# Turning the feed-forward activations on VectorE instead of TensorE, in a two-layer hybrid decoder trunk

## The chip, the cores and the metric

The kernel runs on one core of one Trainium2 chip. The metric is the device time of one execution in microseconds (us). TensorE (PE) multiplies matrices, VectorE (DVE) and ScalarE (ACT) work element by element, GpSimd (POOL) does small jobs and issues some DMAs, and SyncE (SP) issues the loads of the weights. Every engine has its own instruction queue and works through it in order.

## The reference

256 tokens of width 2048 pass through two layers, each a token mixer (gated DeltaNet in layer 0, HGRN2 in layer 1) followed by a SwiGLU feed-forward layer with 5632 inner columns. All arrays are float32. What matters here is the feed-forward layer:

```python
def swiglu(h, w_gate, w_up, w_down):
    return (jax.nn.silu(h @ w_gate) * (h @ w_up)) @ w_down
...
for layer in range(DEPTH):
    ...
    h = h + swiglu(rmsnorm(h, ffn_norm[layer]), ffn_w_gate[layer], ffn_w_up[layer], ffn_w_down[layer])
return rmsnorm(h, final_norm)
```

## The kernel before, in words

**Products of split numbers.** Every float32 operand x is kept as two rounded numbers of the type fp32r, a high part h (x rounded) and a low part l (x - h, rounded), and a product is made of three matmuls: high by high, high by low, low by high. For activations these are the tiles `xt_h`/`xt_l` (input of a layer's first products) and `hth`/`htl` (input of the down projection; the profile's names for `ht` and `lt` in the code). For weights they are `wh`/`wl`.

**The stream of weights.** `stream` walks through all weights in halves of 128x1024 elements (512 KB). SyncE loads a half into one of four `raw` buffers, ScalarE rounds it into `wh`, VectorE subtracts to give `wl` (four split buffers, `SPLIT_BUFS`), and TensorE uses it. In the feed-forward layers each half is used by 12 matmuls with 512 columns (`mm_rows`: two slices of the contraction, two halves of the tokens, three products).

**The feed-forward layer** (`ffn`). There are 22 groups of 256 inner columns, done in two parts of 12 and 10 groups (`FF_PARTS`). A group of gate and up is eight weight halves and fills a PSUM tile `main` (one of two) with tokens on the partitions. When it is complete, `end` runs for both token halves: ScalarE takes the Silu of the gate half into `sg`, and VectorE multiplies the up half by the token's scale and `sg` into `h1` (`h` in the profile). The down projection needs these activations with the inner columns on the partitions. So after every second group, eight 128x128 blocks are transposed on TensorE against the identity (`head` in the profile) into two PSUM banks (`aux`, four in all), and from there split: ScalarE rounds them into `ht`, VectorE subtracts into `lt`. Eleven such pairs make a layer, 22 the kernel. After each part come four groups of the down projection, one for each 512 output columns; each runs over all pairs of that part in order.

**The order of the work.** The program records every operation first (class `Recorder`; this is why nearly every row of the profile has the line L490, the one place that issues them). `plan` then computes an order for each engine: an operation has a price (`COST`; for a VectorE transpose of n elements per partition 0.18 + 0.001 n us, times 1.02), a due time counted back from the main matmuls that need it, and an engine takes the ready operation with the earliest due time. Main matmuls keep their order. The buffers of a tile are taken in that simulated time too. On the chip each engine then follows this fixed order and waits on semaphores.

## Time and profile before

| | |
|---|---|
| median of 3 runs | 2809.66 us (2809.59 to 2812.17) |
| profiled execution, its own time | 2811.11 us |
| span of its instructions | 2809.4 us |
| mean granted TensorE clock | 0.997 |

The profile has one row for each group of equal instructions: line, engine, operation, the names of output and inputs, shapes, count, then busy time in us and the mean of one in ns, and the idle time of that engine before them with the instruction whose end ended it. The chain of work that ended last is followed back from the last instruction, so that a piece of it is time which something would have to replace or remove to change the end. In timeline rows the first number is the start and the second the length, both in us.

### The profile page before, as it was taken

What the parts mean: (1) busy time and instruction counts of PE and PEld (TensorE: products, weight loads), DVE (VectorE), ACT (ScalarE), POOL (GpSimd) and SP (SyncE); (2) the same over time, 40 slices, a digit from 0 to 9 for tenths busy, and PEclk for the clock granted to TensorE, in tenths of its full rate; (3) what the DMA queues carried; (4) which work ended last, traced back from release to release, by engine and by line L of the source; (5) the groups of instructions that cost most, each with busy time, mean ns of one, the idle gap of its engine ahead of it and who ended that gap; (6) DMA issues with size and microseconds to landing.
All of it is one profiled execution on the core that took longest, in us unless ns stands there. A gap on an engine that the chain in (4) does not pass through costs nothing.

```text
span 2809.4 us, 41241 instructions
## 1 busy us (share of the span) xinstructions
PE 2788.2 (99%) x15902; PEld 2376.0 (85%) x15902; DVE 1752.2 (62%) x2543; ACT 1422.0 (51%) x1984; POOL 255.1 (9%) x370
## 2 busy tenths in 40 slices
PE   9999999999999999999999999999999999999998
PEld 9988888888888888888888989988888888888887
DVE  6777888877765545444555687678655454454554
ACT  6646666564554444334444556556454444344443
POOL 1212222223110000000000100000110000000000
PEclk9999999999999999999999999999999999999999
DMA  7686678678776556666556655545775656766564
GB/s 255 198 274 201 197 229 255 209 224 254 230 248 206 192 187 189 224 224 191 190 189 218 214 164 168 170 157 168 235 266 189 192 189 204 224 206 191 189 200 159
DMA packets 162677, 580.54 MB, mean 207 GB/s; under 512 B 20138, under 2 KB 21306, under 8 KB 162352
## 3 DMA queue, kind: packets, MB, share of 16 engines
q1 hardware_dynamic: 138912, 503.15, 55.8%
q0 software_dynamic: 23280, 73.91, 8.4%
q8 instruction: 124, 2.03, 0.3%
q10 hardware_dynamic: 288, 0.85, 0.1%
q14 instruction: 73, 0.60, 0.1%
HBM read 550.52 MB, written 27.31 MB: 206 GB/s over the span
## 4 chain that ended last, share of the span: by engine, by line
PE 98%; issue 0%; ACT 0%; DVE 0%; POOLq 0%; POOL 0%; ACTq 0%
PE main L490 91%; PE aux L490 7%; ACT dec L490 0%; DVE wl L490 0%; ACT wh L490 0%; DVE u L490 0%; ACT xt_h L490 0%; DVE utmp L490 0%; DVE pre L490 0%; ACT y L490 0%; POOLq L1748 0%; ACT junk L490 0%; DVE xl L490 0%; POOL coll L490 0%; DVE xt_l L490 0%
## 5 line engine op out<-in xcount | busy, mean ns | idle before, releaser
L490 DVE TENSOR_TENSOR wl<-raw,wh 128x1024 fp32r<-128x1024 f32 x945 | 1161.4, 1230 | 958.9 <-ACT wh L490 955.9
L490 ACT ACTIVATE wh<-raw 128x1024 fp32r<-128x1024 f32 x945 | 1000.5, 1060 | 1280.2 <-PE main L490 1229.3
L490 PE MATMUL main<-wh,xt_h 128*128 128x512 f32 x2176 | 852.0, 392 | 0.6 <-ACT wh L490 0.6
L490 PE MATMUL main<-wl,xt_h 128*128 128x512 f32 x2176 | 850.4, 391 | 0.9 <-DVE wl L490 0.9
L490 PE MATMUL main<-wh,xt_l 128*128 128x512 f32 x2176 | 850.5, 391 | 0.0
L490 PEld LDWEIGHTS main<-wl,xt_h 128*128 128x128 f32 x2176 | 409.6, 188 | 84.7 <-DVE wl L490 1.3
L490 PEld LDWEIGHTS main<-wh,xt_h 128*128 128x128 f32 x2176 | 409.5, 188 | 84.7 <-ACT wh L490 1.0
L490 PEld LDWEIGHTS main<-wh,xt_l 128*128 128x128 f32 x2176 | 409.5, 188 | 84.5
L490 PE MATMUL main<-xt_h,wl 128*128 128x256 f32 (+1 forms) x1040 | 292.2, 281 | 1.6 <-DVE wl L490 1.6
L490 PE MATMUL main<-xt_l,wh 128*128 128x256 f32 (+1 forms) x1040 | 291.8, 281 | 0.3 <-DVE xt_l L490 0.3
L490 PE MATMUL main<-xt_h,wh 128*128 128x256 f32 (+1 forms) x1040 | 290.3, 279 | 0.0
L490 PE MATMUL main<-wh,hth 128*128 128x512 f32 x664 | 258.7, 390 | 0.0
L490 PE MATMUL main<-wh,htl 128*128 128x512 f32 x664 | 258.6, 389 | 0.0
L490 PE MATMUL main<-wl,hth 128*128 128x512 f32 x664 | 258.3, 389 | 0.0
L490 PEld LDWEIGHTS main<-xt_h,wh 128*128 128x128 f32 (+1 forms) x1040 | 195.6, 188 | 0.3
L490 PEld LDWEIGHTS main<-xt_h,wl 128*128 128x128 f32 (+1 forms) x1040 | 193.8, 186 | 2.2 <-DVE wl L490 2.0
L490 PEld LDWEIGHTS main<-xt_l,wh 128*128 128x128 f32 (+1 forms) x1040 | 193.8, 186 | 0.9 <-DVE xt_l L490 0.5
L490 PE MATMUL main<-wl,ot_h 128*128 128x512 f32 x384 | 150.8, 393 | 0.0
L490 PE MATMUL main<-wh,ot_l 128*128 128x512 f32 x384 | 150.6, 392 | 0.0
L490 PE MATMUL main<-wh,ot_h 128*128 128x512 f32 x384 | 150.5, 392 | 0.0
L490 PEld LDWEIGHTS main<-wh,htl 128*128 128x128 f32 x664 | 124.7, 188 | 25.9
L490 PEld LDWEIGHTS main<-wh,hth 128*128 128x128 f32 x664 | 124.7, 188 | 25.8
(207 smaller groups left out, 2203.0 us busy)
## 6 DMA issues: line engine op xcount, KB each, us to landing
raw<-in_ffn_gu SPq DMA_DIRECT2D x352, 512.0 KB, 4.6
raw<-in_ffn_d SPq DMA_DIRECT2D x176, 512.0 KB, 4.6
raw<-in_hgrn_in SPq DMA_DIRECT2D x128, 512.0 KB, 3.9
raw<-in_gdn_kq SPq DMA_DIRECT2D x64, 512.0 KB, 5.0
raw<-in_gdn_v SPq DMA_DIRECT2D x64, 512.0 KB, 4.6
raw<-in_gdn_z SPq DMA_DIRECT2D x64, 512.0 KB, 5.0
raw<-in_gdn_out SPq DMA_DIRECT2D x64, 512.0 KB, 4.6
x_home<-x POOLq DMA_DIRECT2D x36, 512.0 KB, 5.7
```

The lines of the kernel that those rows point to most:

```text
L490: getattr(getattr(tc.nc, op.eng), op.method)(*args, **kw)
```

## The change

The activations of two groups now share one `h1` tile of 128x2x512 (two buffers instead of four of half the size). VectorE turns it: a transpose instruction of VectorE turns each 32x32 block of its operand, and one instruction takes the blocks from one quarter of the partitions (32 of 128) to another, eight blocks at a time (128x2x512 has 16 combinations of a source quarter and a target quarter, so there are 16 instructions for a pair). The result lies in a new SBUF tile, `turned`. The rounding on ScalarE and the subtraction on VectorE then read `turned`, with one instruction each for the whole pair instead of two. The transposes on TensorE for these tiles and the use of two `aux` banks for them are gone.

```diff
+    def turn(self, out, x):
+
+        out = out.rearrange("p n (t a s) -> p t n a s", t=2, s=32)
+        x = x.rearrange("p t (n b s) -> p t n b s", n=4, s=32)
+        for a in range(4):
+            for b in range(4):
+                self.nc.vector.transpose(
+                    out[32 * b : 32 * b + 32, :, :, a, :], x[32 * a : 32 * a + 32, :, :, b, :]
+                )
...
             def end(ps):
-                h1 = self.tile(self.pool, [P, 2, T], "h1", bufs=4)
+                if gi % 2 == 0:
+                    h1s[gi // 2] = self.tile(self.pool, [P, 2, 512], "h1", bufs=2)
+                h1 = h1s[gi // 2]
                 for tt in range(2):
...
                     nc.vector.scalar_tensor_tensor(
-                        out=h1[:, tt, :], in0=ps[:, tt, T:512], scalar=col, in1=sg,
-                        op0=ALU.mult, op1=ALU.mult,
+                        out=h1[:, tt, gi % 2 * T : (gi % 2 + 1) * T], in0=ps[:, tt, T:512], scalar=col,
+                        in1=sg, op0=ALU.mult, op1=ALU.mult,
                     )
-                h1s[gi] = h1
                 if gi % 2 == 0:
                     return
-                pair = hts[gi // 2] = tuple(
+                turned = self.tile(self.pool, [P, 4, T], "turned", bufs=2)
+                self.turn(turned, h1)
+                hts[gi // 2] = ht, lt = tuple(
                     self.tile(self.pool, [P, 4, T], f"ht{x}", F32R, bufs=max(FF_PARTS) // 2) for x in "hl"
                 )
-                two = self.aux(), self.aux()
-                nc.together(*two)
-                for of, tr in enumerate(two):
-                    for k in range(2):
-                        for tt in range(2):
-                            nc.tensor.transpose(
-                                tr[:, k * T + tt * P : k * T + (tt + 1) * P],
-                                h1s[gi - 1 + of][:, tt, k * P : (k + 1) * P], self.ident,
-                            )
-                for of, tr in enumerate(two):
-                    ht, lt = (t[:, 2 * of : 2 * of + 2, :].rearrange("p a t -> p (a t)") for t in pair)
-                    nc.scalar.activation(ht, tr, AF.Copy)
-                    nc.vector.tensor_tensor(out=lt, in0=tr, in1=ht.bitcast(F32), op=ALU.subtract)
+                nc.scalar.activation(ht, turned, AF.Copy)
+                nc.vector.tensor_tensor(out=lt, in0=turned, in1=ht.bitcast(F32), op=ALU.subtract)
```

## The prediction

> **What bounds the kernel now.** I read the engines' busy times first, then the chain that ended last, then the groups with shapes kept apart, then the timeline of single pairs, and last the waits of the DMA queue.

> ```profile
> span 2809.4 us, 41241 instructions
> PE 2788.2 (99%) x15902; PEld 2376.0 (85%) x15902; DVE 1752.2 (62%) x2543; ACT 1422.0 (51%) x1984; POOL 255.1 (9%) x370
> ...
> PE 98%; issue 0%; ACT 0%; DVE 0%; POOLq 0%; POOL 0%; ACTq 0%
> ```

> TensorE is the bound nearly everywhere: it is busy for 99% of the span and is 98% of the chain that sets the end. VectorE idles 38% of the time. So the question of this change is what TensorE time leaves the chain, and whether VectorE, loaded with the work instead, ever makes TensorE wait. The two feed-forward layers in the chain, in order of time (start, length, work; the eleven pieces of the first layer's pairs run from the first row to the tenth, and the last row is the last pair of the second layer):

> ```profile
> 891.58 0.87 PE aux L490 x8
> 892.45 43.54 PE main L490 x192
> 935.99 0.87 PE aux L490 x8
> 936.86 43.54 PE main L490 x192
> 980.40 0.88 PE aux L490 x8
> 981.28 43.54 PE main L490 x192
> 1024.82 0.87 PE aux L490 x8
> ...
> 1466.27 0.88 PE aux L490 x8
> ...
> 2695.15 0.87 PE aux L490 x8
> ```

> The reader is to see a metronome. Two groups of gate and up are 192 matmuls in 43.54 us, 0.2268 us each; then eight transposes take 0.87 us; and nothing lies between. The period of a pair is 44.41 us (935.99 less 891.58). One weight half is 12 matmuls, 2.72 us.

> ```profile
> L490 DVE TENSOR_TENSOR wl<-raw,wh 128x1024 fp32r<-128x1024 f32 x945 | 1161.4, 1230 | 958.9 <-ACT wh L490 955.9
> L490 ACT ACTIVATE wh<-raw 128x1024 fp32r<-128x1024 f32 x945 | 1000.5, 1060 | 1280.2 <-PE main L490 1229.3 <-issue 11.3 <-PE aux L490 8.3
> ...
> L490 DVE TENSOR_TENSOR htl<-aux,hth 128x512 fp32r<-128x512 f32 x44 | 28.2, 682 | 0.0
> ...
> L490 ACT ACTIVATE hth<-aux 128x512 fp32r<-128x512 f32 x44 | 23.5, 587 | 0.0
> ...
> L490 PE MATMUL aux<-head,h 128*128 128x128 f32 x176 | 22.8, 272 | 0.0
> ...
> L490 DVE STREAM_TRANSPOSE inv<-u 32x256 f32<-32x256 f32 x32 | 13.8, 432 | 1.8 <-DMA u<-u_dram 0.6 <-ACT u L490 0.4
> ```

> The columns are the count, the busy time, the mean of one in ns, and the idle time before them. wh and wl are the rounded weight half and its remainder, made on ScalarE and VectorE for every half of the stream: 1.06 and 1.23 us. The 176 transposes are the 22 pairs by eight. The DeltaNet layer already has VectorE transposes of the size that the change adds, 32x256 in f32.

> **The change, step by step.** (1) *Removed from TensorE*: 22 batches of eight transposes. Each batch takes 0.87 us of the chain, with the switch into it and out of it, since the main matmuls on both sides are complete (192 in 43.54 us, with the first slow matmul after a switch inside). 22 x 0.87 = 19.1 us, or 19.2 us with the two or three that show 0.88. All of it lies on the path, because TensorE waits for nothing there. The row of the group offers two other sums: 22.8 us busy (1.04 a batch, which overlaps the neighbouring matmuls), and 176 x 272 ns = 47.9 us (durations of instructions that overlap in the pipeline). I take the chain's number, which is a distance between neighbours.

> [...]

> (2) *Added to VectorE*: 16 transposes of 32x256 per pair, 352 in all. The nearest rows are three in a row in the DeltaNet layer:

> ```profile
> 196.86 1.36 DVE L490 STREAM_TRANSPOSE inv<-u 32x256 f32<-32x256 f32 x3
> 198.25 0.19 DVE L490 TENSOR_TENSOR u<-u,utmp 128x29 f32<-128x29 f32 x1
> ```

> That is 0.453 us each, start to start. So a pair costs 16 x 0.453 = 7.25 us. The new ones have one more level of stride on each side; the trace has no such instruction. From below I bound one by 0.19 us (the small sum above), from above by 1.23 us (the wl row, a VectorE instruction of four times as many elements on each partition). I take 0.453, the row of the same operation, size and type.

> (3) *Changed on VectorE and ScalarE*: two subtractions of 128x512 (2 x 682 ns) become one of 128x1024 from SBUF (1.23 us like wl), and two rounding copies of 128x512 (2 x 587 ns) become one of 128x1024 (1.06 us like wh): 0.1 us less per pair on each engine. VectorE's busy time rises by 22 x (16 x 0.432 + 1.23 - 1.36) = 149 us, to some 1901 us; a pair's window holds

> ```profile
> 891.58:935.99 44.41, 44.41 (x202) 36.86 (x201) 22.39 (x22) 19.41 (x22) 0.00 (x0) 1.00 0.60 191
> ```

> 22.39 us of VectorE in 44.41 now, and 22.4 + 7.25 - 0.1 = 29.5 in 43.54 after, 68%. ScalarE stays at 19.3. The granted clock here is 1.00 and has nothing to give.

> (4) *What covers the added 7.25 us.* VectorE runs in order, and behind the turns stand the wl subtractions that TensorE needs. The steady state:

> ```profile
> 1478.08 1.06 ACT L490 ACTIVATE wh<-raw 128x1024 fp32r<-128x1024 f32 x1 [1.66 <-PE main L490]
> 1480.80 1.06 ACT L490 ACTIVATE wh<-raw 128x1024 fp32r<-128x1024 f32 x1 [1.66 <-PE main L490]
> ...
> 1476.45 1.23 DVE L490 TENSOR_TENSOR wl<-raw,wh 128x1024 fp32r<-128x1024 f32 x1 [1.49 <-ACT wh L490]
> 1479.17 1.23 DVE L490 TENSOR_TENSOR wl<-raw,wh 128x1024 fp32r<-128x1024 f32 x1 [1.49 <-ACT wh L490]
> ```

> wh starts when TensorE has left a split buffer, wl ends 2.32 us later (1478.08 to 1480.40), and with four buffers (SPLIT_BUFS) that half is wanted three halves after the release, 8.2 us: wl may be 5.8 us late before TensorE notices. VectorE idles 1.49 us in each half before wl; three turns (1.36 us) fit into it without moving wl, so the 16 need some six halves of the 16 that a pair has. If one starts just as wl becomes ready, wl is 0.45 us late. A late wl also returns its raw buffer late:

> ```profile
> raw<-in_ffn_gu SPq DMA_DIRECT2D x352, 512.0 KB, 4.6
> SPq L490 <- DVE wl L490: 1908.9, 772, 12.8
> ```

> SP waits on wl for its next load, which lands 4.6 us later (1485.0 for the wl above) and is wanted four halves after its predecessor's wh (1488.96): 3.9 us to spare. Both covers hold if wl slips by 0.5 us. If they were gone, each microsecond of lateness beyond 5.8 would be one on the chain, per pair.

> (5) *Added wait*: the ScalarE copy of a pair waits for all 16 turns, and wh stands behind it in ScalarE's queue; the subtraction then waits for the copy, with wl behind. Priced alike: a copy put too early would delay wh out of the same 5.8 us. The order (plan) ranks work by due time, and the turned pair is due only in the down projection.

> (6) *Where the due time is near*: the last pair of the second part of each layer. Its down group starts while the pair is still being made:

> ```profile
> 1460.66 0.39 PE L490 MATMUL main<-wh,hth 128*128 128x512 f32 x1
> ...
> 1463.10 0.87 DVE L490 SCALAR_TENSOR_TENSOR h<-main,rstd,sg 128x256 f32<-128x256 f32 x2
> 1464.67 1.23 DVE L490 TENSOR_TENSOR wl<-raw,wh 128x1024 fp32r<-128x1024 f32 x1 [0.71 <-ACT wh L490]
> ```

> The last pair is used from the ninth half on, 1460.66 + 8 x 2.72 = 1482.4. From 1463.97, one turn fits before the wl of 1464.67 and three after each wl: the last ends near 1478.3, the copy behind a wh near 1480.2, the subtraction behind a wl near 1481.6. That is 0.8 us early even with every wl first; the due times let the turns overtake a wl or two before that. Cost nothing, at worst some 2 us in each of two places.

> (7) *PSUM and SBUF*: two of the four aux banks are no longer borrowed for a pair; h1 keeps its 8 KB per partition (2 x 4 KB for 4 x 2 KB), turned adds 8 KB. Cost nothing. (8) *The order elsewhere* is computed anew from the first pair on, so the HGRN2 layer may be dealt a little differently; TensorE's own waits there are

> ```profile
> PE aux L490 <- issue: 6.2, 4, 2.0
> ```

> 6.2 us in four. I take no change, and 6 us each way for the range.

> *Sum*: 19.2 us off the chain, nothing on it. The profiled execution took 2811.11 us around its span of 2809.4; the median of the runs is 2809.66, 1.45 us lower, and I subtract from that: 2790.4 us, 0.68% less.

> **The rivals.** *A, the turns stand in a block.* If the 16 turns, the wait for the copy and the subtraction are placed in one run ahead of a wl, that wl is late by 7.25 + 1.06 + 1.23 - 1.49 = 8.05 us, 2.2 more than the 5.8 of cover: 22 x 2.2 = 48 us on the chain, 29 net, 2839 us. It decides slower from 6.7 us of lateness (5.8 + 0.87). For it: one in-order queue, and the 16 become ready at once. Against: due times rank a wl ahead of turns that are wanted much later.

> [...]

> *B, a turn with these strides is slow.* At p us each, three per half (as the order prices them, at 0.44) put VectorE (3p - 1.49) behind in each of 5.3 halves. It ends slower from p = 0.91, and at the upper bound of 1.23 costs 5.9 us a pair net of the cover of 5.8, 22 x 5.9 = 130 less 19: 2920 us. For it: the trace has no turn with these strides. Against: the same operation at 0.453.

> *C, the gain is eaten*: TensorE waits where it transposed, for a wl 6.4 to 6.9 us late, or the HGRN2 layer gets worse by as much: about 2810 us. For it: nothing in the waits.

> *D, more than the chain shows*: a removed transpose gives back its whole duration, 47.9 us, 2762 us. For it: the mean of 272 ns in its row. Against: the distance of the neighbouring matmuls leaves only 0.87 us per batch. [...]

> **How the numbers follow.** Forecast 0.82; A 0.05, B 0.04, C 0.05, D 0.04. This kernel's measurement tells some 0.2%, 5.6 us, from no change. Faster holds the forecast and D, 0.86; same is C, 0.05; slower A and B, 0.09. The range is 19.2 us less 6 to plus 6: 2784 to 2797, with the two late pairs (4 us) inside; it leaves out the 0.18 of the rivals.

> **What would show it.** Right: the chain of the changed kernel has pieces of main matmuls in the feed-forward layers with no aux piece at the pairs, a pair's period of 43.54 us, 352 STREAM_TRANSPOSE of turned at about 0.43 us, VectorE near 1901 us busy, TensorE near 2769, and no idle time of main matmuls there behind wl. Step 2 is wrong if a turn is over 0.9 us; step 4 if TensorE waits for wl in these layers; step 6 if main waits for the last pair near the ninth half of a second part; step 8 if the HGRN2 layer's length moves by over 2 us.

## The result, and the profile after

The changed kernel takes 2781.37 us (median of 4 runs, 2779.86 to 2782.76), the kernel before 2810.39 us in the same comparison (2809.59 to 2812.17): a ratio of 0.9896, 95% interval 0.9879 to 0.9913. The forecast was 2790.4 us with a range of 2784 to 2797. The direction was right, but the gain is 29 us where 19.2 were forecast, and the time lies 2.6 us below the range.

The head of the profile of the changed kernel, its group of turns, and the row of the DMA queue that brings instructions:

```profile
span 2780.4 us, 41201 instructions
PE 2764.4 (99%) x15726; PEld 2354.9 (85%) x15726; DVE 1904.7 (69%) x2873; ACT 1421.1 (51%) x1962; POOL 252.6 (9%) x370
...
q8 instruction: 123, 2.02, 0.3%
...
L490 DVE STREAM_TRANSPOSE turned<-h 32x256 f32<-32x256 f32 x352 | 153.5, 436 | 7.2
```

TensorE's busy time fell by 23.8 us (2788.2 to 2764.4), less than the span (29.0). So part of the gain is idle time that went away, in a kernel where TensorE was 99% busy. Where it went is read from the chain that ended last, by taking the same pieces of work in both kernels. First the chain of the kernel before (start, length, work):

```profile
844.90 0.87 PE aux L490 x8
...
1576.37 0.87 PE aux L490 x8
...
1652.30 1.86 PE aux L490 x148
1654.16 2.01 issue
...
1656.55 11.11 PE main L490 x48
...
1753.54 1.69 PE aux L490 x141
1755.23 1.67 issue
...
1757.39 12.71 PE main L490 x48
...
1855.52 1.62 PE aux L490 x97
1857.14 1.93 issue
...
1859.71 12.52 PE main L490 x47
...
1958.39 1.51 PE aux L490 x94
1959.90 0.56 issue
...
1961.20 10.88 PE main L490 x47
...
2038.46 0.87 PE aux L490 x8
...
2772.20 24.50 PE aux L490 x108
```

And the chain of the changed kernel:

```profile
844.78 0.87 PE aux L490 x8
845.65 636.50 PE main L490 x2808
...
1566.43 0.87 PE aux L490 x8
...
1642.36 1.51 PE aux L490 x122
1643.86 0.70 issue
...
1645.30 11.12 PE main L490 x48
...
1742.30 2.00 PE aux L490 x165
1744.30 11.13 PE main L490 x48
...
1840.85 2.06 PE aux L490 x119
1842.91 10.89 PE main L490 x47
...
1939.97 2.06 PE aux L490 x121
1942.03 10.89 PE main L490 x47
...
2019.30 0.87 PE aux L490 x8
...
2743.22 24.49 PE aux L490 x108
```

Four landmarks divide the time: the transposes ahead of the first feed-forward layer (844.90, after: 844.78), the last ones ahead of the mixing in the HGRN2 layer (1576.37, 1566.43), those behind it (2038.46, 2019.30), and the long last piece (2772.20, 2743.22). The changed kernel leads by 0.12, 9.94, 19.16 and 28.98 us at them. So each feed-forward layer gave 9.82 us, close to what the prediction said (19.2 for both, where 19.6 came), and **the HGRN2 layer, which the change doesn't touch, gave 9.22 us**.

Inside that layer the same four places differ. Each of its four head groups has a burst of small matmuls into `aux`, and behind the burst 47 or 48 main matmuls. From the start of a burst to the start of those main matmuls, the kernel before takes 4.25, 3.85, 4.19 and 2.81 us, the changed one 2.94, 2.00, 2.06 and 2.06: 6.04 us less. The pieces behind it take 12.71 and 12.52 us in two of the four before, and 11.13 and 10.89 after: 3.21 us less. Together this is 9.25, all of the layer's gain. "issue" in the chain is time in which TensorE waits for nothing that the profile shows.

The longer pieces have a halved clock, 0.50 from 1758.18 to 1761.59 and from 1860.58 to 1863.99. The kernel before in a stretch behind the second burst (length, busy time and count of TensorE, its weight loads, VectorE, ScalarE and GpSimd, then the granted clock; the last two numbers are the DMA engines' share and GB/s):

```profile
1757.40:1761.50 4.10, 4.10 (x12) 3.19 (x13) 3.32 (x9) 1.06 (x1) 0.00 (x0) 0.60 0.33 111
```

The mean clock is 0.60, and 12 matmuls fall into these 4.1 us; 19 fall into the 4.0 us from 1762.00 on, at a clock of 1.00.

### The profile page after: what moved, and what is told of

Read it like the earlier page. It is cut to its first block, busy times and chain, and to the rows that moved or that the text cites. A ratio compares the mean times of both kernels' runs of the same rounds, so it can differ in the third digit from the quotient of the medians.

```text
span 2780.4 us, 41201 instructions
## 1 busy us (share of the span) xinstructions
PE 2764.4 (99%) x15726; PEld 2354.9 (85%) x15726; DVE 1904.7 (69%) x2873; ACT 1421.1 (51%) x1962; POOL 252.6 (9%) x370
## 4 chain that ended last, share of the span: by engine, by line
PE 99%; ACT 0%; DVE 0%; issue 0%; POOLq 0%; POOL 0%; ACTq 0%
PE main L490 92%; PE aux L490 7%; ACT dec L490 0%; DVE wl L490 0%; ACT wh L490 0%; DVE u L490 0%; ACT xt_h L490 0%; DVE utmp L490 0%; DVE pre L490 0%; ACT y L490 0%; POOLq L1750 0%; ACT junk L490 0%; DVE xl L490 0%; POOL coll L490 0%; DVE xt_l L490 0%
## 5 line engine op out<-in xcount | busy, mean ns | idle before, releaser
L490 DVE TENSOR_TENSOR wl<-raw,wh 128x1024 fp32r<-128x1024 f32 x945 | 1161.9, 1230 | 775.5 <-ACT wh L490 767.2
L490 ACT ACTIVATE wh<-raw 128x1024 fp32r<-128x1024 f32 x945 | 1000.6, 1060 | 1250.1 <-PE main L490 1166.5
L490 PE MATMUL main<-wl,xt_h 128*128 128x512 f32 x2176 | 849.2, 390 | 0.9 <-DVE wl L490 0.9
L490 PE MATMUL main<-wh,xt_h 128*128 128x512 f32 x2176 | 849.1, 390 | 0.6 <-ACT wh L490 0.6
L490 PE MATMUL main<-wh,xt_l 128*128 128x512 f32 x2176 | 849.4, 390 | 0.0
L490 PEld LDWEIGHTS main<-wh,xt_h 128*128 128x128 f32 x2176 | 408.6, 188 | 84.9 <-ACT wh L490 1.0
L490 PEld LDWEIGHTS main<-wl,xt_h 128*128 128x128 f32 x2176 | 408.6, 188 | 84.7 <-DVE wl L490 1.2
L490 PEld LDWEIGHTS main<-wh,xt_l 128*128 128x128 f32 x2176 | 408.7, 188 | 84.2
L490 PE MATMUL main<-xt_h,wl 128*128 128x256 f32 (+1 forms) x1040 | 292.2, 281 | 1.5 <-DVE wl L490 1.5
L490 PE MATMUL main<-xt_l,wh 128*128 128x256 f32 (+1 forms) x1040 | 291.9, 281 | 0.3 <-DVE xt_l L490 0.3
L490 PE MATMUL main<-xt_h,wh 128*128 128x256 f32 (+1 forms) x1040 | 290.3, 279 | 0.0
L490 PE MATMUL main<-wh,htl 128*128 128x512 f32 x664 | 258.6, 389 | 0.0
L490 PE MATMUL main<-wl,hth 128*128 128x512 f32 x664 | 258.4, 389 | 0.0
L490 PE MATMUL main<-wh,hth 128*128 128x512 f32 x664 | 258.4, 389 | 0.0
L490 PEld LDWEIGHTS main<-xt_h,wh 128*128 128x128 f32 (+1 forms) x1040 | 195.7, 188 | 0.3
L490 PEld LDWEIGHTS main<-xt_h,wl 128*128 128x128 f32 (+1 forms) x1040 | 193.8, 186 | 2.0 <-DVE wl L490 1.9
L490 PEld LDWEIGHTS main<-xt_l,wh 128*128 128x128 f32 (+1 forms) x1040 | 193.8, 186 | 0.9 <-DVE xt_l L490 0.5
L490 DVE STREAM_TRANSPOSE turned<-h 32x256 f32<-32x256 f32 x352 | 153.5, 436 | 7.2
L490 PE MATMUL main<-wl,ot_h 128*128 128x512 f32 x384 | 150.8, 393 | 0.0
L490 PE MATMUL main<-wh,ot_l 128*128 128x512 f32 x384 | 150.6, 392 | 0.0
L490 PE MATMUL main<-wh,ot_h 128*128 128x512 f32 x384 | 150.5, 392 | 0.0
L490 PEld LDWEIGHTS main<-wh,hth 128*128 128x128 f32 x664 | 124.7, 188 | 25.9
## 6 DMA issues: line engine op xcount, KB each, us to landing
raw<-in_ffn_gu SPq DMA_DIRECT2D x352, 512.0 KB, 3.7
raw<-in_ffn_d SPq DMA_DIRECT2D x176, 512.0 KB, 4.7
raw<-in_hgrn_in SPq DMA_DIRECT2D x128, 512.0 KB, 3.7
raw<-in_gdn_kq SPq DMA_DIRECT2D x64, 512.0 KB, 4.9
raw<-in_gdn_v SPq DMA_DIRECT2D x64, 512.0 KB, 4.5
raw<-in_gdn_z SPq DMA_DIRECT2D x64, 512.0 KB, 5.0
raw<-in_gdn_out SPq DMA_DIRECT2D x64, 512.0 KB, 4.8
x_home<-x POOLq DMA_DIRECT2D x36, 512.0 KB, 5.2
```

The source lines that it names most:

```text
L490: getattr(getattr(tc.nc, op.eng), op.method)(*args, **kw)
```

## The experiments

**Theories.** By the first, the HGRN2 layer's gain comes from *where its bursts stand in TensorE's stream of instructions*. A burst is 384 instructions (192 matmuls, each with its weight load) in 2.0 us, 5.2 ns an instruction. The instruction queue of the kernel before carries 124 packets in 2.03 MB, 16,384 bytes each; TensorE's 31,915 instructions in the trace are 124.7 times 256. Counting all of TensorE's instructions in the trace, its four "issue" waits stand 1,792 apart, which is 7 x 256, and the one of the changed kernel stands 256 ahead of the first of them (18,625 and 18,881 instructions from the start). The theory reads this as a stream in blocks of 256, each fetched when the one ahead of it is begun: a burst that meets two block edges, 1.3 us apart at 5.2 ns an instruction, would run dry at the second. In the first three bursts a packet starts 0.8 to 1.0 us after the first edge (in the fourth, whose wait is the shortest, 0.25 us ahead of it) and lands about 1 us later, and TensorE resumes 1.3 to 1.5 us after that. The change takes 176 TensorE instructions (88 transposes with their weight loads) out ahead of this layer and so moves all four bursts against the blocks. The rivals: the order of the work, computed anew, came out better in the layer; or the freed `aux` banks let its work start earlier. Comparing the orders, all engines' sequences in the HGRN2 layer are the same in both kernels, but for the order of the small matmuls within the third and fourth burst, which speaks against the first rival, but not against the second.

The place of a burst is told below as the number of its instructions ahead of the first block edge in it, with an edge every 256 instructions from those at the waits. It is 91, 69, 50 and 27 for the four bursts before, and 10, -12, 225 and 202 after (a negative number: the edge lies that far ahead of the burst). This counts from a burst's first matmul. The third and fourth burst begin with some 21 matmuls of 16 columns:

```profile
1855.45 0.37 PE L490 MATMUL aux<-qp,kp 128*32 128x16 f32 x21
```

The expectations below count these two bursts from the first matmul of 48 columns, which comes only then, and so have their places some 42 instructions off; those of the first two are right.

### What moves the HGRN2 layer

**e3_both_turns**: VectorE's turns stay, and TensorE's transposes come back beside them; nothing reads their results.

```diff
                 turned = self.tile(self.pool, [P, 4, T], "turned", bufs=2)
                 self.turn(turned, h1)
+                two = self.aux(), self.aux()
+                nc.together(*two)
+                ... the eight transposes of the kernel before, from h1
```

> The changed kernel, with the eight TensorE transposes of each pair kept (into two aux banks that nobody reads) beside the 16 VectorE turns, so that VectorE and ScalarE do the changed kernel's work and TensorE that of the kernel before. If VectorE's added 7 us per pair cost nothing and everything that was won was TensorE's, it takes what the kernel before takes, about 2810 us, with 44.41 us per pair and 498.3 us in the HGRN2 layer (block theory). The rival, that the HGRN2 layer gained from the other engines' timing, has 44.41 us per pair and 489 us in that layer, about 2801 us.

Measured: 2809.71 us against 2811.84, 0.9992 [0.9983, 1.0001]. The whole gain is gone, in both places: the first feed-forward layer takes 647.2 us as before, and in HGRN2 the four waits are back. So VectorE's 16 turns and the other buffers by themselves cost and give nothing, and all of the 29 us hangs on TensorE's transposes. It doesn't yet tell instructions from `aux` banks.

**e8_before_pad30 and e9_after_pad44** tell them apart: tiny matmuls are added in one place ahead of the HGRN2 layer, and nothing else is touched. Each is four instructions of TensorE (two matmuls and two weight loads in float32: 44 of them make up for the 88 transposes that are gone, 9,398 matmuls in both of the rows below). 30 of them in the kernel before are 120 instructions and move its bursts to the places -29, -51, 186 and 163, outside the stretch that costs anything; 44 in the changed kernel are 176 and bring back the places of before.

```diff
+PADS = 30      # 44 in the changed kernel
...
+                if op is self.padded:     # ahead of the last transposes of the layer's input
+                    for _ in range(PADS):
+                        tc.nc.tensor.matmul(
+                            args[0][0:32, 0:16], args[2][:, 0:32], args[2][:, 0:16], start=True, stop=True
+                        )
```

> The kernel before with 30 of the tiny matmuls (four instructions and 0.068 us each by the runs with 20, 40 and 88 of them, so 120 instructions and 2.0 us) ahead of the last transposes in front of the HGRN2 layer. Block theory: the four bursts then start 29, 51, 112 and 135 instructions behind an edge, no wait is left, the layer takes 451.9 us between its transposes instead of 462.1, the pads add 2.0 us before it, and the kernel takes about 2802.2 us, 0.3% less. Rival (the layer got shorter in the changed kernel through the timing of the other engines): 462.1 us, and about 2812.4 us.

> The changed kernel with 44 of the tiny matmuls (176 instructions, 3.0 us) at the same place, as many instructions as the first feed-forward layer lost. Block theory: the four bursts start 166, 188, 249 and 16 instructions behind an edge as in the kernel before, the waits come back, the layer takes about 462.1 us between its transposes instead of 452.9, and the kernel about 2793.6 us. Rival: 452.9 us, and about 2784.4 us.

Measured: the kernel before with 30 matmuls more takes 2803.06 us against 2812.45, 0.9966 [0.9953, 0.9978]; its HGRN2 layer takes 452.0 us instead of 462.1, and its chain runs through the first burst without a wait:

```profile
1652.30 2.02 PE aux L497 x165
1654.31 11.11 PE main L497 x48
```

The changed kernel with 44 more takes 2793.65 us, 0.9934 [0.9922, 0.9947]; its layer takes 462.6 us. TensorE's waits of that kernel (time, count, longest):

```profile
PE aux L497 <- issue: 6.8, 4, 2.2
```

The same two programs counted by stretches whose edges lie in the four waits (length, then busy time and count of TensorE and of its weight loads). First the kernel before, then the changed kernel with 44 matmuls:

```profile
0.00:1655.00 1655.00, 1649.17 (x9398) 1406.37 (x9399) 1080.05 (x1774) 874.93 (x1308) 220.87 (x330) 1.00 0.68 216
1655.00:1756.00 101.00, 99.06 (x893) 90.43 (x893) 77.08 (x108) 59.02 (x80) 3.66 (x3) 1.00 0.52 167
```

```profile
0.00:1645.80 1645.80, 1639.39 (x9398) 1398.01 (x9398) 1156.28 (x1939) 874.54 (x1297) 220.00 (x330) 1.00 0.68 217
1645.80:1746.50 100.70, 99.06 (x893) 90.41 (x893) 77.05 (x109) 59.01 (x80) 3.66 (x3) 1.00 0.52 168
```

Two programs that do different work up to there, nine microseconds apart, wait behind the same number of matmuls. That decides it: adding work that nothing needs made the kernel before 9.4 us faster, and took away 12.3 us of the changed kernel's gain (10.7 by the two ratios; in the profiles 9.8 in the layer and 3.0 for the matmuls themselves). The `aux` banks were free in e9 and not in e8, and the layer went the other way in both.

**e1_before_pad40, e2_after_pad88, e4_after_pad20** are the same edit with 40, 88 and 20 matmuls, run before I knew that each counts four instructions; the expectations count two, so their places are wrong.

> The kernel before with 40 tiny TensorE matmuls (80 instructions, about 0.5 us) put ahead of the last transposes that stand in front of the HGRN2 layer; no engine's order changes otherwise. Block theory (TensorE gets its instructions in blocks of 256, and a dense burst that reaches the edge of a block soon after the edge before it stands still until the next block has come): 80 instructions more leave the same place in the block as the 176 fewer of the changed kernel, so the HGRN2 layer falls from 498.3 us to 489.1 + 0.5, the 6.2 us of waits for nothing fall to about 0.7, and the kernel takes about 2801.7 us. Rival (the layer got shorter because VectorE, ScalarE or the loads arrive otherwise after the turned pairs): nothing of that is changed here, so the layer stays at 498.3 + 0.5 us and the kernel takes about 2811 us.

> The changed kernel with 88 such tiny matmuls (176 instructions, about 1.1 us) at the same place, as many instructions as the first feed-forward layer lost. Block theory: the HGRN2 layer has the places of the kernel before again, 498.3 + 1.1 us, with waits of 2.0, 1.7, 1.9 and 0.6 us in its four bursts, and the kernel takes about 2791.7 us. Rival: the layer stays near 489.1 + 1.1 us, and the kernel takes about 2782.5 us.

> The changed kernel with 20 tiny matmuls (40 instructions, 0.25 us) ahead of the HGRN2 layer. Block theory: the one wait that is left there (0.70 us, a block's edge 266 instructions into the burst of 384, the edge before it 10 into it) goes, because the edges move 40 instructions towards the front, to 226 and to 30 ahead of the burst; the layer takes 489.1 - 0.7 to 1.3 + 0.25 us and the kernel about 2780.7 us, a gain too small for the time to tell but plain in the layer's length. Rival: 489.1 + 0.25 us, the wait of 0.7 us stays.

Measured: 2807.18 us (0.9983 [0.9974, 0.9992]), 2792.97 (0.994 [0.9927, 0.9952]) and 2786.21 (0.9908 [0.9895, 0.9922]), all against 2811.84. e1 and e4 miss by 5.5 us each; e2 came within 1.3 us by coincidence. By the right count, e1 puts the edges at 187, 165, 146 and 124, and only the last burst waits (1.7 us; layer 454.2 us); in e4 only the last does, at 123 (1.8 us; 455.8); in e2 the last two, at 129 and 107 (1.9 and 1.8 us; 459.4). So the misses gave more places on the scale. The 14 traces hold 56 bursts. In 24 of them the first edge lies at 10 to 129, and every one of these waits, 0.56 to 2.41 us. In the other 32 it lies at 145 to 244 (a place of -12 has its next edge at 244), and none of these waits but the first of e6, which stands right behind empty instructions (below). By the theory, two edges fit into a burst of 384 only where the first lies at 0 to 128, which agrees. The waits under 1.4 us are at 10, 27 and 28, where the packet starts about at the edge, up to 0.25 us ahead of it, and one at 90 (e7); in e3 the packet starts 1.5 us behind an edge at 28, and the wait is 2.4 us.

**e5_after_place30, e6_before_place30, e7_after_place165**: the first burst is put at a chosen place of the block by empty instructions (41, 122 and 176 of them in the traces).

```diff
+                if op is self.burst:      # ahead of the first burst's first matmul
+                    tc.nc.tensor.addr_align(256, offset=PLACE)
```

> The changed kernel with one directive ahead of the first of the four dense bursts of the HGRN2 layer: it fills TensorE's instruction stream up (40 empty instructions) so that the burst starts 30 instructions behind the edge of a block of 256. No engine's work or order changes. Block theory: the four bursts start 30, 52, 113 and 136 instructions behind an edge, no burst of 384 meets a second edge before its end is near (226 instructions and fewer to the first one), the wait of 0.7 us goes, the layer takes about 452.0 us between its transposes instead of 452.9, and the kernel about 2780.5 us. Rival (the waits hang on something else than the place in the stream): 452.9 us.

> The kernel before with the same directive (121 empty instructions): the feed-forward layers keep their TensorE transposes. Block theory: all four waits of the HGRN2 layer (6.2 us) and the halved clock behind two of them go, the layer takes about 452.0 us between its transposes instead of 462.1, and the kernel about 2800.3 us, 10 us or 0.36% less. Rival: nothing but empty instructions is added, so 462.1 us and about 2810.4 us or a little more.

> The changed kernel with the directive set to 165 instructions behind an edge (175 empty instructions), where the kernel before has its first burst. Block theory: the four waits come back (2.0, 1.7, 1.9 and 0.6 us, each with or without the halved clock behind it), the layer takes about 462.1 us between its transposes, and the kernel about 2790.6 us. Rival: the layer stays at 452.9 us and the kernel at about 2781.4 us.

Measured against 2812.15: e5 2780.88 us (0.9893 [0.9879, 0.9906]), with no "issue" wait left and the layer at 451.9 us; e6 2809.97 (0.9991 [0.9982, 1.0000]); e7 2802.13 (0.9969 [0.9958, 0.998]). e5 is the lowest time of all, but not to be told from the changed kernel (0.9896). e7 has the four waits again, as meant. e6 missed by 10 us and e7 by 11.5: the bursts two to four of e6 do run through, but empty instructions aren't free. The traces have one every 71 ns (the median), 9.0 us for the 122 of e6 and 13.0 us for the 176 of e7. TensorE's earlier matmuls cover the first 4.2 us of them, and it stands still for the rest, 5.0 and 9.0 us; behind that the clock is halved for 6.8 us in e6. The 41 of e5 take 3.1 us, all of it covered.

### How thick the cover in the feed-forward layers is

**e11_turn_twice**: each of the 16 turns is made twice, 14.5 us of VectorE in each pair.

```diff
-                self.turn(turned, h1)
+                for _ in range(2):
+                    self.turn(turned, h1)
```

> The changed kernel with every turn done twice into the same tile (704 transposes on VectorE, 14 us per pair). If VectorE's work is free as long as it fits, 36.4 us of VectorE in 43.54 per pair cost nothing there, and only the last pair of each layer's second part can come late, by up to some 5 us in each of two places: 2781 to 2791 us. Rival (each further turn costs TensorE something, by memory traffic or by late wl): 7 us per pair at the worst, about 2930 us.

Measured: 2800.32 us against 2812.45, 0.9955 [0.9941, 0.9968], slower than expected by 9 us or more. The chain of its first part of the feed-forward layer, and VectorE near the last pair of the second part:

```profile
844.54 263.42 PE main L490 x1162
```

```profile
1466.40 9.80 DVE L490 STREAM_TRANSPOSE turned<-h 32x256 f32<-32x256 f32 x21
1476.23 2.36 DVE L490 TENSOR_TENSOR wl<-raw,wh 128x1024 fp32r<-128x1024 f32 x2
```

1,162 main matmuls in 263.42 us are 0.2267 us each: inside the pairs twice the work on VectorE still costs nothing. The loss is at the last pair of each part, where down needs the pair soon: TensorE waits there for `hth` and `htl`, 12.4 us in six waits (1.7 us at the end of a first part, 4.5 at the end of a second part), and in the second part runs at half clock behind it (0.50 from 1480 to 1485 us). The first layer's feed-forward chain is 9.9 us longer for it (646.4 us to 636.5).

**e10_turn_block**: the order is computed with a turn priced at 0.001 us, so that all 16 stand in one row; the chip does the same work.

```diff
                 self.nc.vector.transpose(...)
+                self.nc.ops[-1].cost = 0.001
```

> The changed kernel with a price of nearly nothing for a turn in the order's planning, so that the 16 turns of a pair stand in one row on VectorE (with the same place for TensorE's instructions). By the prediction's cover, wl comes 16 x 0.44 - 1.49 = 5.5 us late and may be 5.8 us late: no wait of TensorE, 43.54 us per pair, and about 2781.4 us. Rival (the cover is a half smaller than worked out, 3.1 us): 2.4 us per pair on the chain, 53 us in all, about 2834 us.

Measured: 2800.12 us against 2812.45, 0.9958 [0.9943, 0.9973], 18.7 us above the expectation. From the first main matmul behind the input to the first transposes of down, the first layer takes 646.17 us instead of 636.50: 0.88 us in each pair, behind a wait for `wl` (22 of the kernel's 24 such waits). I took the ScalarE copy for the cause, since it was planned early and would hold up `wh` behind it; e12 tests that.

**e12_block_late_copy**: as e10, with the last turn's planned delay raised to 7.0 us, so that the copy stands behind three more `wh`.

```diff
+                self.nc.ops[-1].cost = 0.001
+        self.nc.ops[-1].lag = 7.0
```

> The block of 16 turns again, with ScalarE's copy of the pair planned 7 us later, so that three more wh stand ahead of it in ScalarE's queue; VectorE's row of 16 is unchanged. If the 0.88 us per pair that the block costs came from the wh that were shut in behind the waiting copy (step 5 of the prediction), TensorE's waits for wl in the feed-forward layers go and a pair takes 43.5 us: about 2781 us. Rival (the cover of 5.8 us for a late wl is smaller than worked out): the waits stay, 44.4 us per pair, about 2800 us.

Measured: 2800.97 us against 2811.32, 0.9957 [0.994, 0.9973]. The copy did move, and the waits stayed (14.4 us in 24), so that theory fell. VectorE of this kernel shows the cause:

```profile
977.26 0.87 DVE L490 SCALAR_TENSOR_TENSOR h<-main,rstd,sg 128x256 f32<-128x256 f32 x2
978.17 7.18 DVE L490 STREAM_TRANSPOSE turned<-h 32x256 f32<-32x256 f32 x16
985.38 4.63 DVE L490 TENSOR_TENSOR wl<-raw,wh 128x1024 fp32r<-128x1024 f32 x4
```

with TensorE's next matmul on that `wl`:

```profile
986.66 0.50 PE L490 MATMUL main<-wl,xt_h 128*128 128x512 f32 x1 [0.56 <-DVE wl L490]
```

The `wh` of that half starts at 977.75, and `wl` normally 1.09 us later (1478.08 to 1479.17 in the prediction's rows), at 978.84. It starts at 985.38, 6.54 late, and TensorE waits 0.56: the cover is 6.0 us, not unlimited, and the block overran it because it begins right behind `h`, without the idle time ahead of a `wl` that I had counted on.

## Why the prediction was right in direction and wrong in size

- **Step 1** (22 batches of 0.87 us off TensorE) held. A pair of the changed kernel:

```profile
891.58:935.10 43.52, 43.52 (x194) 36.05 (x193) 29.30 (x38) 19.38 (x22) 0.00 (x0) 1.00 0.59 194
```

TensorE is busy for all of the 43.52 us that a pair now takes, where it took 44.41: 0.89 each, 19.6 us for 22. Rival D, 47.9 us, is out: the two layers gave 9.82 each.
- **Steps 2 and 3** held. VectorE between two pairs:

```profile
976.91 1.23 DVE L490 TENSOR_TENSOR wl<-raw,wh 128x1024 fp32r<-128x1024 f32 x1 [0.24 <-ACT wh L490]
978.16 1.34 DVE L490 STREAM_TRANSPOSE turned<-h 32x256 f32<-32x256 f32 x3
979.63 1.23 DVE L490 TENSOR_TENSOR wl<-raw,wh 128x1024 fp32r<-128x1024 f32 x1
980.88 1.78 DVE L490 STREAM_TRANSPOSE turned<-h 32x256 f32<-32x256 f32 x4
982.70 1.22 DVE L490 TENSOR_TENSOR wl<-raw,wh 128x1024 fp32r<-128x1024 f32 x1
```

Four turns in 1.78 us are 0.45 each from start to start, as taken; rival B is out. VectorE is busy for 1904.7 us (predicted 1901), 29.3 in a pair (29.5).
- **Step 4** (the cover) held. The turns of this pair stand in rows of one to four ahead of a `wl`, over six halves for the 16. A `wl` comes at most 0.35 us late (982.70, where 2.72 us after 979.63 would be 982.35; predicted 0.45), and no wait of TensorE follows. The 5.8 us of cover measured 6.0 in e12. Rival A is real as a mechanism: forced, the block costs 0.88 us a pair, all that the change gains there. It was priced too high (2.2 us a pair, from 8.05 us of lateness where 6.54 came), and the order doesn't make it.
- **Step 5** (the added wait on ScalarE) cost nothing, and in e12 moving that copy changed nothing.
- **Step 6** held with more room than forecast: `htl` of the last pair is done at 1469.93 in the changed kernel, and is wanted some 3.5 us later (the down group starts at 1451.62, plus eight halves of 2.72), where 0.8 was forecast. e11 shows that this is the thinnest place, as the step said.
- **Step 8 is the step that failed**: "The order elsewhere is computed anew ... I take no change, and 6 us each way". The layer moved by 9.22 us. I read the row of 6.2 us "issue" in four waits and bounded the change by its size, but named the wrong cause: the order in that layer is the same, but within two bursts. What changed is the count of instructions ahead of it: the first layer's eleven batches of step 1 are 88 transposes with 88 weight loads, 176 instructions. And 6 us was too small a bound, since a wait also costs the slow start behind it (6.04 us in the bursts for 5.5 us less of waits) and, in two of four, a half clock (3.21 us). Rival C had this layer in it, but with the loss as its only sign.

That the places explain the waits is shown by e8 and e9. Behind which waits the clock halves, one of 1.67 us and not one of 2.01, can be read from the traces' clock; the reason they don't show. Apart from the kernel's end it halves in them for 3.41 us or a multiple of it, and the halvings of one trace start whole numbers of 3.41 us apart (1758.18 and 1860.58 in the kernel before, 30 times). Three stretches of that grid in the kernel before (the first two hold most of the wait of 2.01 us and all of that of 1.67, and the third follows the second):

```profile
1652.37:1655.78 3.41, 1.79 (x172) 1.69 (x167) 2.44 (x4) 0.12 (x1) 0.00 (x0) 1.00 0.48 148
1754.77:1758.18 3.41, 1.75 (x90) 1.51 (x79) 2.06 (x5) 0.00 (x0) 0.00 (x0) 1.00 0.79 252
1758.18:1761.59 3.41, 3.41 (x10) 2.64 (x9) 2.68 (x8) 1.06 (x1) 0.00 (x0) 0.50 0.16 62
```

The wait of 2.01 us runs over from its stretch into the next, and 1.62 us of it are idle time of the first; the other lies within one stretch, 1.66 us. The wait of 1.93 us has 1.90 us of idle time in one stretch, and a clock of 0.50 in the next. From 850 to 2770 us of all 14 traces, every stretch at full clock with 1.76 us or more of idle TensorE is followed by one at 0.50, and none with 1.62 us or less; of the four between, two are. What separates those four stays open.

## What to carry to other kernels

Here an edit that took 176 TensorE instructions out of one layer took 9.22 us off a later one that it doesn't touch, where bursts of 384 instructions run at 5.2 ns each; 120 instructions more, of no use to the result, took 10.1 us off the same layer (e8). "issue" waits came and went without any change of that stage. So look for regular "issue" waits before costing an edit, count the instructions between them (1,792 here), and give such a stage a range of waits plus slow restart plus half clock, in both directions (here 6.0 us for the first two and 3.2 for the last). A small difference of two versions may be this placing alone: shift one of them by a hundred or so instructions, as e8 and e9 do (120 and 176), before crediting it to the edit.

## What the runs showed of the hardware that was not expected

A wait of 1.67 us was already followed by a half clock: 1.66 us of it lie in one stretch of a grid of 3.41 us, and the next stretch has a clock of 0.50. The wait of 2.01 us has 1.62 us in one stretch, and the next has 1.00.

And a row of eight blocks in float32 was turned across the partition quarters by VectorE in 0.44 us (436 ns, the mean of 352), so that the full transpose of 128x2x512 took 7.2 us (16 turns in 7.18 us in e12) of an engine that had 22 us idle in each pair.
